# Expert stage with gathered tokens and returned rows by indirect DMA, experts interleaved, and four more weight tiles

## The chip, the cores and the metric

One Trainium2 chip (trn2), one of its cores. The metric is device time in microseconds (us) of one execution. Engines are named as in the profile: PE (TensorE products), PEld (its weight loads), DVE (VectorE), ACT (ScalarE), POOL (GpSimd), SP (SyncE, which issues most DMAs).

## The reference

Two transformer blocks on 512 tokens of 1024 features in fp32. Block 1 mixes by convolution, neighbourhood attention and a gated delta net, and then has a mixture of experts; block 2 has attention and a feed-forward layer. The change lies in the experts of block 1. Of `_hier_moe`, cut to what matters (the last lines in words):

```python
pg = jax.nn.softmax((xt @ wg + bg), axis=-1)            # 4 groups
grp = jnp.argmax(pg, axis=-1)
el_grp = (xt @ we + be).reshape(n, 4, 8)[own group]     # 8 experts of a group
top_logit, top_e = lax.top_k(el_grp, 2)
gate = pg_top * jax.nn.softmax(top_logit, axis=-1)
# of each token's two experts e: y += gate * ((silu(x @ w1[e]) * (x @ w3[e])) @ w2[e])
```

There are 32 experts, w1 and w3 of 1024x512 and w2 of 512x1024. Each of the 512 tokens goes to two experts.

## The kernel before, in words

The expert stage runs from about 474 to 1054 us of the trace. The work of the experts is cut into blocks of 64 token slots. The first four experts (`NPRE`) have one block each at the start; of the others 26 have one block (a unit of 64 slots) and two have two (a unit of 128 slots). Which expert takes which block is a list that the kernel computes at run time from the router; four blocks, 256 slots, are a group (`group`, L1279; `seq_g` gives the groups' order). A loop for tokens beyond the listed blocks (`beyond`, L1574) stands before the seventh group and has no turn here.

Weights come as tiles of 1 MB (128x2048 fp32): two of w1, two of w3 and two of w2 for each expert, 192 in all, issued by SP (`issue`, L1337) in the order in which they are used. Each goes into the next buffer of a ring: three tiles of tag `s`, five of tag `t`, and later two `u`; `WSEQ` gives the ring's order and `U_AT` where `u` comes in. Twelve tiles are loaded ahead, some in memory that is used otherwise later (`pre_issue`, L1363). A load waits until PE has done with what its buffer held.

A group's tokens reach their slots by products. `fill_xs` (L1311) compares each slot's number with the slot keys `K` of the 512 tokens (two keys a token, one for each expert), which gives a one-hot matrix `oh`; for each of eight feature tiles eight products of `oh` with the normed tokens `hN` (in two parts, hi and lo) give the transposed inputs, and `evac_x` puts scale and shift of the norm on them (alternately on DVE and ACT).

An expert (`expert`, L1396) runs two halves of 16 products for w1 and w3 (the unit's inputs are the stationary operand), the SiLU gate (`sil` on ACT, `ge` on DVE), four transposes of `ge`, the copy `gT` on ACT, and 16 products with w2. `evac_y` (L1442) multiplies the result by the gate and a row `G2` and splits it in two parts, `Yh` and `Yl`. The results go back to the tokens by products too: `slot_side` (L1427) makes the one-hot matrix `S` of a pair of units (128 slots), and `scatter_steps` (L1452) runs 16 products of `S` with `Yh` and `Yl` for each pair, whose sums DVE adds to the tokens (`xb`; `big` in the trace), eight steps a pair.

`run_pair` (L1471) sets the order: it runs the two units of a pair one after the other and puts the steps of the next group's inputs and of the last pair's return at fixed places between an expert's parts; the tables `PLAN0` to `PLAN3` say how many at each place. In the last pair a one-element square root (`warm`) has ACT load its table early. Behind the stage stands the norm of block 2: `begin` multiplies the tokens by a row (`xc`), and PE transposes them.

Of the kernel before, what the change touches and what calls it, by code (L numbers as in the profile page):

```python
# [11 lines left out]
I32 = mybir.dt.int32  # L12
# [12 lines left out]
NS, NS2, NS3 = 3, 5, 2                                    # weight tiles: at all times, from the experts on, and late  # L25
XLAG = 2                                                 # tiles of w_out between x1 and its turning
NPRE = 4                                                 # experts that come first, whatever their load
NOV = 2                                                  # experts that get twice the slots
NSG = NE - NPRE - NOV                                    # the others
NB = NSG + 2 * NOV                                       # blocks of 64 slots after the first NPRE  # L30
seq_g = [0, 4, NSG - 2, 8, NSG + 2, 12, 16, 20]          # their groups, the experts with two blocks in turn with others
NLOOP = 6                                                # group of blocks that the loop comes before
LASTP = 22                                               # first block of the last pair
# the experts' weight tiles in the order of their first use (s, t: NS, NS2; x: slots; u: NS3, from the tiles U_AT on)
WSEQ = "sssttttt" + "xx"
U_AT = (11, 12)
# steps of the pair before (outputs' way back) and of the next group (slots) before the four quarters of an expert: the
# first and the second pair, a pair's first and second expert, an expert of two blocks
PLAN0 = [(0, 2), (0, 4), (0, 0), (0, 0)]
PLAN3 = [(0, 1), (0, 1), (4, 2), (4, 2)]  # L40
PLAN2 = [[(0, 1), (0, 0), (2, 1), (2, 1)], [(0, 0), (0, 0), (2, 1), (2, 1)]]
PLAN1 = [(0, 1), (0, 2), (4, 3), (4, 3)]
# [34 lines left out]

TILES = order_tiles(ORD)

# [68 lines left out]
def kernel(ctx: ExitStack, tc: tile.TileContext, a: dict, out, dbg=None, stop=99):  # L148
# [965 lines left out]
    if stop <= 1:  # L1114
        cmn.close()
        return
# [1236 lines left out]
```

## Time and profile before

| | us |
|---|---|
| median of 3 runs | 1889.21 (1883.33 to 1890.45) |
| span of the profiled execution | 1882.1 |
| its own time around the span | not given |
| first expert product to the end of the last one | 473.76 to 1054.11 |
| first transposes of block 2 | 1068.08 |

The profiled execution's span is that from its first to its last instruction; the runs' times hold some launch and end around it. The page's busy shares are averages over both blocks; the stage that the change touches is read by its own windows.

### The profile page before, as it was taken

The numbers are of one execution on the slowest core, as the hardware profiler recorded it, in microseconds if no ns is written. First come the engines' busy times: TensorE is split into PE (matmuls) and PEld (weight loads), VectorE is DVE, ScalarE is ACT, GpSimd is POOL, SyncE is SP. The second block draws the span as 40 slices with busy tenths as digits, with TensorE's granted clock in tenths as the row PEclk, the third lists the DMA queues.
The fourth block names the chain that finished last, engine by engine and source line by source line (L and its number), as shares of the span: only waits on it lengthen the run. The fifth ranks groups of instructions, "written<-read, shape, count | busy, mean of one in ns | idle before, by whom it ended". The sixth has DMA issues, their size and how long they took to land.

```text
span 1882.1 us, 22777 instructions
## 1 busy us (share of the span) xinstructions
PE 1745.2 (93%) x8346; PEld 1208.8 (64%) x8346; DVE 1053.9 (56%) x1959; ACT 683.5 (36%) x1355; POOL 497.6 (26%) x460
## 2 busy tenths in 40 slices
PE   4978989997999999999899799999999999999998
PEld 3757767775444445454443386866688778888886
DVE  7866777764455243544533678755436765425545
ACT  4454543443211111111121554656533454314432
POOL 4364523203111111111111232233202432322251
PEclk7989999998999999999999899999999999999999
DMA  7636234564689887978898457412133332232221
GB/s 286 198 120 218 84 131 136 201 239 188 270 352 401 322 319 270 369 288 326 330 426 349 149 199 262 167 61 86 45 112 117 119 104 104 84 112 90 92 99 45
DMA packets 90177, 370.20 MB, mean 197 GB/s; under 512 B 19680, under 2 KB 42704, under 8 KB 49744
## 3 DMA queue, kind: packets, MB, share of 16 engines
q1 hardware_dynamic: 90064, 368.72, 53.1%
q8 instruction: 67, 1.10, 0.2%
q14 instruction: 46, 0.38, 0.1%
HBM read 359.23 MB, written 9.46 MB: 196 GB/s over the span
## 4 chain that ended last, share of the span: by engine, by line
PE 42%; DVE 4%; ACT 2%; DMA 1%; issue 1%; POOL 1%; DVEq 0%; SPq 0%; ACTq 0%; POOLq 0%
PE b L186 37%; PE b L1906 1%; PE b L1807 1%; PE b L1894 1%; DVE adascr L189 1%; DMA ws<-in_wada_dram 1%; DVE big L192 1%; ACT junk L1634 0%; ACT wh L342 0%; DVE wl L192 0%; PE b L1731 0%; DVE big L189 0%; DMA crow<-in_crow_dram 0%; PE b L2100 0%; POOL hF L192 0%
## 5 line engine op out<-in xcount | busy, mean ns | idle before, releaser
L186 PE MATMUL b<-ws,xs 128*64 128x512 f32 (+1 forms) x896 | 253.2, 595 | 2.0 <-DVEq L1583 2.0
L192 POOL TENSOR_TENSOR wl<-ws,wh 128x1024 fp32r<-128x1024 f32 (+1 forms) x60 | 142.7, 2380 | 377.6 <-ACT wh L342 360.8
L342 ACT CAST wh<-ws 128x1024 fp32r<-128x1024 f32 (+1 forms) x154 | 151.8, 993 | 219.8 <-PE b L186 182.7
L192 POOL TENSOR_TENSOR Yl<-y,Yh 64x512 fp32r<-64x512 f32 (+1 forms) x60 | 77.7, 1315 | 479.0 <-ACT Yh L342 479.0
L186 PE MATMUL b<-hF,wh 128*128 128x512 f32 x656 | 202.2, 389 | 0.0
L186 PEld LDWEIGHTS b<-ws,xs 128*64 128x64 f32 (+1 forms) x896 | 85.3, 140 | 152.1 <-issue 149.3
L192 DVE TENSOR_TENSOR wl<-ws,wh 128x1024 fp32r<-128x1024 f32 (+1 forms) x94 | 115.9, 1237 | 90.7 <-ACT wh L342 87.6
L186 PE MATMUL b<-hB,wh 128*128 128x512 f32 x512 | 164.3, 401 | 0.0
L192 DVE TENSOR_TENSOR big<-big,b 128x512 f32<-128x512 f32 x136 | 89.3, 683 | 114.2 <-PE b L186 113.4
L189 DVE SCALAR_TENSOR_TENSOR adascr<-ws,crow 128x1024 bf16<-128x1024 f32 x96 | 135.6, 1412 | 9.0 <-DMA ws<-in_wada_dram 8.0
L186 PEld LDWEIGHTS b<-hF,wh 128*128 128x128 f32 x656 | 123.1, 188 | 25.5
L186 PE MATMUL b<-hT,wh 128*128 128x512 f32 x384 | 132.8, 424 | 0.0
L186 PE MATMUL b<-ws,gT 128*64 128x512 f32 (+1 forms) x496 | 122.1, 606 | 6.5 <-ACT gT L1416 6.5
L186 PE MATMUL b<-hF,wl 128*128 128x512 f32 x328 | 127.6, 389 | 0.0
L186 PEld LDWEIGHTS b<-hB,wh 128*128 128x128 f32 x512 | 96.7, 193 | 23.5 <-issue 1.8
L189 DVE SCALAR_TENSOR_TENSOR u<-b,cols,u 128x511 f32<-128x511 f32 x88 | 65.8, 748 | 79.3 <-ACT u L2181 77.8
L189 DVE SCALAR_TENSOR_TENSOR y<-b,gsl,G 64x512 f32<-64x512 f32 (+1 forms) x64 | 48.0, 750 | 98.6 <-PE b L186 66.6
L186 PE MATMUL b<-hB,wl 128*128 128x512 f32 x256 | 101.6, 397 | 0.0
L342 ACT CAST Yh<-y 64x512 fp32r<-64x512 f32 (+1 forms) x64 | 39.5, 617 | 169.1 <-DVE y L189 169.1
L186 PEld LDWEIGHTS b<-oh,hN 128*128 128x128 f32 x576 | 77.2, 194 | 20.2 <-issue 16.5
L186 PE MATMUL b<-wh,gf 128*128 128x512 f32 x288 | 88.7, 389 | 0.0
L1409 ACT ACTIVATE sil<-b 64x512 f32<-64x512 f32 (+1 forms) x32 | 18.9, 591 | 189.8 <-PE b L186 189.8
(483 smaller groups left out, 3433.9 us busy)
## 6 DMA issues: line engine op xcount, KB each, us to landing
ws<-in_ew_dram SPq DMA_DIRECT2D x188, 1024.0 KB, 7.3
ws<-in_wada_dram SPq DMA_DIRECT2D x48, 1024.0 KB, 5.0
ws<-in_w_upT_dram SPq DMA_DIRECT2D x22, 1024.0 KB, 4.9
ws<-in_w_in2T_dram SPq DMA_DIRECT2D x16, 1024.0 KB, 4.8
ws<-in_w_inT_dram SPq DMA_DIRECT2D x12, 1024.0 KB, 5.1
ws<-in_w_downN_dram SPq DMA_DIRECT2D x8, 1024.0 KB, 4.9
ws<-in_w_outT_dram SPq DMA_DIRECT2D x4, 1024.0 KB, 4.8
ws<-in_w_v_dram SPq DMA_DIRECT2D x4, 1024.0 KB, 5.2
```

Source lines behind the costliest of these rows:

```text
L186: nc.tensor.matmul(o, l, r, start=start, stop=stop)
L189: return nc.vector.scalar_tensor_tensor(o, i0, s, i1, op0=op0, op1=op1, **kw)
L192: (eng or nc.vector).tensor_tensor(o, i0, i1, op)
L342: nc.scalar.copy(hi, src)
L1409: nc.scalar.activation(s_, b[0][r[0], :], AF.Silu)
L1807: nc.tensor.matmul(o[j], x_[k][:, t], w_[:, i], start=k == 0 and n == 0 and j % 2 == 0, stop=k == KT - 1 and n == 2, skip_group_check=True)
L1894: nc.tensor.transpose(tp[:, k * P:(k + 1) * P], sp[:, k * P:(k + 1) * P], ident)
L1906: nc.tensor.matmul(po[64 * g_:64 * g_ + 64, k * P:], v[k][:, 64 * h:64 * h + 64], PT[g_][:, PO[k]:PO[k] + T - k * P], start=k == 0, stop=k ...
```

## The change

Token vectors move by indirect DMAs. The normed tokens are written to DRAM (`ud`) by ACT's queue. `fill_xs` compares slots and keys as before (eight compares, one for each key), but multiplies the one-hot matrices by columns of two numbers only: 16 small products for a group give each slot's token number and its row in the return buffer. DVE turns them into integers, POOL's queue gathers 128 rows of 4 KB for each half of a group (`xg`; empty slots lie out of bounds and are skipped), and PE transposes the tile, 16 transposes a group.

Results are only multiplied by `G2` into a tile `Y`, which POOL's queue scatters to `yd` in DRAM (`send`), a pair at a time. Near the end `come_back` reads `yd` in four 1 MB tiles on POOL's queue, and eight DVE steps add gate times row to the tokens. The last pair still goes through `S` and products. The loop for tokens beyond the list moves to the same scheme.

Units are interleaved (`run`): a unit's first half, then the previous unit's transposes of `ge`, the unit's second half, then the previous unit's w2 products. The w2 tiles are issued one unit later (`order_w`). The ring has 13 tiles that are used in turn (five `t`, one `k`, three `s`, four new `e`), one more (`x`) that is used once, and later two `u`; 14 tiles are loaded ahead. The early square root is left out. `PLAN_F` says where a unit's place holds steps of the next group's inputs.

```diff
-WSEQ = "sssttttt" + "xx"
-U_AT = (11, 12)
...
+NE4 = 4
+NLATE = 11
+WSEQ = "tttttkxssseeee"
+U_AT = (15, 16)
+PLAN_F = {0: [(0, 0, 0, 0), (0, 1, 1, 0), (1, 1, 1, 1), (1, 1, 1, 1)],
+          4: [(1, 0, 1, 0), (0, 0, 0, 0), (1, 1, 1, 1), (1, 1, 1, 1)],
+          3: [(1, 0, 1, 0), (1, 1, 1, 1), (1, 1, 1, 1)],
+          1: [(1, 1, 0, 4)]}
...
+    ud = dpool.tile([T, D], F32, name="ud")
+    yd = dpool.tile([2 * T, D], F32, name="yd")
...
+    xg = [EX.tile([P, D], F32, name="xg%d" % h) for h in range(2)]
...
-            nc.scalar.activation(u, v, AF.Copy, scale=rs[:, j:j + 1])
-            split(hi, lo, u, nc.gpsimd)
+            nc.scalar.activation(u, xb[:, j, f_], AF.Copy, scale=rs[:, j:j + 1])
+            nc.scalar.dma_start(ud[j * P:(j + 1) * P, f_], u)
...
-    def fill_xs(slots, xs):
-        oh = c4("oh", [P, NTT, 256])
+    def fill_xs(slots, xs, nh, r_, np_, ix):
+        w = nh * P
+        oh = [EX.tile([P, NTT, 256], F32R, tag="oh", name=nm("oh"), bufs=2) for _ in range(2)]
         for j in range(NTT):
-            t = M.tile([P, 256], F32, tag="oht", name=nm("oht"), bufs=2)
-            ts_(t, slots, K[:, 1, j:j + 1], None, OP.is_equal)
-            last[0] = stt(oh[:, j], slots, K[:, 0, j:j + 1], t, OP.is_equal, OP.add)
+            for i in range(2):
+                ts_(oh[i][:, j, :w], slots[:, :w], K[:, i, j:j + 1], None, OP.is_equal)
+        yield
+        n = r_.shape[3]
+        b = bank()[:, :2 * n].rearrange("p (h n) -> p h n", h=2)
+        for h in range(nh):
+            for j in range(NTT):
+                for i in range(2):
+                    mm(b[:, h], oh[i][:, j, h * P:(h + 1) * P], r_[:, j, i], j == 0 and i == 0, j == NTT - 1 and i == 1)
...
+        nc.vector.tensor_copy(sc[:, :nh], b[:, :nh])
+        ts_(e[:, :nh], sc[:, :nh, 0], 0.0, 4096.0, OP.is_equal, OP.mult)
+        stt(gi[:, :nh], sc[:, :nh, 0], -1.0, e[:, :nh], OP.add, OP.add)
+        tt(e[:, :nh], e[:, :nh], sc[:, :nh, 1], OP.add)
+        last[0] = stt(ri[:, :nh], sc[:, :nh, 0], -1.0, e[:, :nh], OP.add, OP.add)
+        ix["ri"], ix["sc"] = ri, sc
+        for h in range(nh):
+            nc.gpsimd.indirect_dma_start(out=xg[h][:np_], out_offset=None, in_=ud[:, :],
+                                         in_offset=bass.IndirectOffsetOnAxis(ap=gi[:np_, h:h + 1], axis=0),
+                                         bounds_check=T - 1, oob_is_err=False)
         yield
...
-            for j in range(NTT):
-                for q in range(2):
-                    mm(b, hN[q][j][m // 4][:, (m % 4) * P:(m % 4 + 1) * P], oh[:, j], j == 0 and q == 0,
-                       j == NTT - 1 and q == 1)
-            evac_x(xs[:, m], b, m)
+            w = (nh - 1) * P + np_
+            for h in range(nh):
+                nc.tensor.transpose(b[:, h * P:h * P + np_], xg[h][:np_, m * P:(m + 1) * P], ident[:np_, :np_])
+            evac_x(xs[:, m, :w], b[:, :w], m)
             yield
...
+    def send(Y, ri, h, np_=P):
+        nc.gpsimd.indirect_dma_start(out=yd[:, :], out_offset=bass.IndirectOffsetOnAxis(ap=ri[:np_, h:h + 1], axis=0),
+                                     in_=Y[:np_], in_offset=None, bounds_check=2 * T - 1, oob_is_err=False)
...
+        skip += "e" if nis[0] > 6 * NE - NLATE else ""
...
+    def order_w(us_):
+        for i, u in enumerate(us_):
+            for q in range(2):
+                yield from wreq(u, q)
+            if i:
+                yield from wreq(us_[i - 1], 2)
+        yield from wreq(us_[-1], 2)
...
+    def evac(b, Y, r):
+        for q in range(2):
+            f_ = slice(q * 512, (q + 1) * 512)
+            tt(Y[r, f_], b[q], G2[r, f_], OP.mult)
...
+    def results(u, b):
+        ps_, r = u["pair"], u["rows"]
+        if u["last"]:
+            if "Y" not in ps_:
+                ps_["S"], ps_["Y"] = slot_side(made[ps_["grp"]][2]["sc"][:, ps_["h"]]), \
+                    [EX.tile([P, D], F32R, tag="oh", name=nm("Yp"), bufs=2) for _ in range(2)]
+            evac_y(b, *ps_["Y"], ps_["S"][1], r)
+            if r.stop == P:
+                late.append((*ps_["Y"], ps_["S"][0]))
+            return
+        if "Y" not in ps_:
+            ps_["Y"] = out_tile()
+        evac(b, ps_["Y"], r)
+        if r.stop == P:
+            send(ps_["Y"], made[ps_["grp"]][2]["ri"], ps_["h"])
+    def run(us_):
+        prev = None
...
+        for u in us_:
+            h = u.get("hook", lambda i: None)
+            h(0)
+            x = expert(u["xs"](), u["sl"], u)
             next(x)
-            if leng is None and i == 1:
-                tc.keep_in_program_order(nc.scalar.activation(small.tile([P, 1], F32, tag="warm", name=nm("warm")),
-                                                              ones[:, 0:1], AF.Sqrt))
...
+            h(1)
+            if prev:
+                next(prev[1])
+            h(2)
+            next(x)
+            h(3)
+            if prev:
+                results(prev[0], next(prev[1]))
+                if "after" in prev[0]:
+                    prev[0]["after"]()
+            prev = u, x
+        end(prev)
...
+    def come_back():
+        for j in range(NTT):
+            t = EX.tile([P, 2048], F32, tag="we", name=nm("yb"), bufs=NE4).rearrange("p (i f) -> p i f", i=2)
+            nc.gpsimd.dma_start(t, yd.rearrange("(i j p) f -> j p i f", i=2, j=NTT)[j])
+            for i in range(2):
+                stt(xb[:, j], t[:, i], gt[:, i, j:j + 1], xb[:, j], OP.mult, OP.add)
...
+    flat_us[-5]["after"] = zero_rows
+    flat_us[-3]["after"] = come_back
+    run(flat_us[n0:])
```

The order of instructions moves on PE, on POOL and at the stage's end on DVE.

On PE the first unit of before alternates its w1 (`kg`) and w3 (`ws`) products on its inputs (`xf`):

```order
L186 MATMUL b_4069<-kg_3997,xf_3995 64x512
L186 MATMUL b_4070<-ws_3999,xf_3995 64x512
L186 MATMUL b_4069<-kg_3997,xf_3995 64x512
L186 MATMUL b_4070<-ws_3999,xf_3995 64x512
L186 MATMUL b_4069<-kg_3997,xf_3995 64x512
```

In the middle of the program, now, a unit runs them in fours (`x4`), and the transposes of gathered tokens (`xg`) and of the previous unit's `ge` stand between its two halves:

```order
L188 MATMUL b_4956<-we_4968,xs_4442 64x512 x4
L188 MATMUL b_4957<-ws_1141_4970,xs_4442 64x512 x4
L1365 MATMUL b_4980<-ident,xg_3993 128x128
L1365 MATMUL b_4980<-ident,xg_3994 128x128
L1459 MATMUL b_4984<-ident,ge_4932 128x64 x4
L1365 MATMUL b_4991<-ident,xg_3993 128x128
L1365 MATMUL b_4991<-ident,xg_3994 128x128
```

Of the 30 units of 64 slots, 17 alternated before, 9 ran in fours and 4 were mixed; now 10 alternate and 20 run in fours.

On POOL before, the start of the expert stage held the splits of normed tokens (`hN`) and of results (`Yl`):

```order
L192 TENSOR_TENSOR hN_3962<-xr_3991,hN_3954 128x512
L192 TENSOR_TENSOR Yl_4255<-y_4256,Yh_4254 64x512
L192 TENSOR_TENSOR Yl_4255<-y_4260,Yh_4254 64x512
L192 TENSOR_TENSOR Yl_4255<-y_4303,Yh_4254 64x512
L192 TENSOR_TENSOR Yl_4255<-y_4307,Yh_4254 64x512
```

On POOL now, the same place holds the gathers (`ud` by the indices `gi`) and the sends (a pair's `y` to `yd` by `ri`):

```order
L1307 MEMSET xg_3994 128x1024
L1357 DMA xg_3993<-ud,gi_4080 128x1024
L1357 DMA xg_3994<-ud,gi_4080 128x1024
L1357 DMA xg_3993<-ud,gi_4269 128x1024
L1357 DMA xg_3994<-ud,gi_4269 128x1024
L1371 DMA yd<-y_3997,ri_4081 1024x1024
L1357 DMA xg_3993<-ud,gi_4503 128x1024
L1357 DMA xg_3994<-ud,gi_4503 128x1024
L1371 DMA yd<-y_4437,ri_4081 1024x1024
```

Both kinds stand in one queue: a send behind the next group's gathers where its results come later.

At the end of the stage DVE before had the last pair's sums in pairs of steps (`big<-big,b`) around the two evacuations of the last unit (`y`):

```order
L192 TENSOR_TENSOR ge_8007<-sil_8006,b_7981 64x512
L192 TENSOR_TENSOR big<-big,b_8027 128x512
L192 TENSOR_TENSOR big<-big,b_8031 128x512
L189 SCALAR_TENSOR_TENSOR y_8049<-b_8035,gsl_7921,G_3495 64x512
L189 SCALAR_TENSOR_TENSOR y_8053<-b_8036,gsl_7921,G_3495 64x512
```

Now the eight sums of the returned rows (`yb`) stand there, the first two ahead of the last unit's `ge` and the others ahead of or between the evacuations of the last pair (`y`, split into `Yp`):

```order
L191 SCALAR_TENSOR_TENSOR big<-yb_6878,gt,big 128x1024 x2
L194 TENSOR_TENSOR ge_6938<-sil_6937,b_6895 64x512
L198 TENSOR_SCALAR S_6955<-tokr,sc_6462 128x512
L191 SCALAR_TENSOR_TENSOR big<-yb_6882,gt,big 128x1024 x2
L191 SCALAR_TENSOR_TENSOR big<-yb_6886,gt,big 128x1024 x2
L191 SCALAR_TENSOR_TENSOR big<-yb_6890,gt,big 128x1024
L191 SCALAR_TENSOR_TENSOR y_6961<-b_6941,gsl_6957,G_3536 64x512
L191 SCALAR_TENSOR_TENSOR big<-yb_6890,gt,big 128x1024
L194 TENSOR_TENSOR Yp_6960<-y_6961,Yp_6959 64x512
```

The last unit's `ge`, and with it its transposes and w2 products, now stands behind the first read of returned rows on DVE. Behind the stage the order on every engine is as before.

## Rows read from the trace of the kernel before

**Rows 1.** Windows of the expert stage, with two stretches inside it.
```profile
core 0: us, PE busy (x) PEld busy (x) DVE busy (x) ACT busy (x) POOL busy (x), PEclk, DMA share, GB/s
474.00:1055.00 581.00, 554.72 (x2481) 259.11 (x2477) 256.73 (x479) 92.83 (x169) 77.74 (x60) 1.00 0.85 330
540.00:620.00 80.00, 77.78 (x379) 36.55 (x374) 37.69 (x67) 12.74 (x23) 13.01 (x10) 1.00 1.00 402
940.00:1000.00 60.00, 58.72 (x282) 25.84 (x280) 23.14 (x41) 10.47 (x19) 10.00 (x8) 1.00 1.01 426
```

**Rows 2.** Waits of SP's queue, whole span: us in total, times, longest.
```profile
SPq L182 <- PE b L186: 415.1, 151, 12.7
```

**Rows 3.** Groups of PE by form, 440 to 1075: busy us, mean ns | idle.
```profile
L186 PE MATMUL b<-ws,xs 128*64 128x512 f32 x832 | 225.0, 595 | 2.0 <-DVEq L1583 2.0
L186 PE MATMUL b<-ws,gT 128*64 128x512 f32 x464 | 108.0, 607 | 6.5 <-ACT gT L1416 6.5
L186 PE MATMUL b<-oh,hN 128*128 128x256 f32 x576 | 82.7, 290 | 2.4 <-DVE oh L189 2.4
L186 PE MATMUL b<-Yh,S 128*128 128x512 f32 x136 | 59.8, 441 | 3.0 <-ACT Yh L342 3.0
...
L186 PE MATMUL b<-ws,xf 128*64 128x512 f32 x112 | 28.9, 596 | 0.0
...
L1414 PE MATMUL b<-ident,ge 64*128 64x64 f32 x120 | 13.8, 235 | 14.1 <-DVE ge L192 13.0
...
L186 PE MATMUL b<-sel,pls 128*128 128x36 f32 x8 | 1.1, 279 | 0.0
L260 PE MATMUL b<-ident,K 128*128 128x128 f32 x8 | 1.0, 272 | 0.0
```

**Rows 4.** Timeline of PE in two units: start us, us, instructions.
```profile
494.38 7.03 PE L186 MATMUL b<-ws,xf 128*64 128x512 f32 x32
...
665.28 5.37 PE L186 MATMUL b<-ws,xs 128*64 128x512 f32 x16
...
672.66 5.42 PE L186 MATMUL b<-ws,xs 128*64 128x512 f32 x16
```

**Rows 5.** Timeline of the stage's start, DVE and PE.
```profile
466.77 0.62 DVE L196 TENSOR_SCALAR oht<-pat,K 128x256 f32<-128x256 f32 x2
...
467.92 5.91 PE L186 MATMUL b<-oh,hN 128*128 128x256 f32 x32 [2.44 <-DVE oh L189]
...
473.76 0.64 PE L186 MATMUL b<-kg,xf 128*64 128x512 f32 x1
```

**Rows 6.** Timeline of PE at the stage's end.
```profile
1050.46 3.65 PE L186 MATMUL b<-ws,gT 128*64 128x512 f32 x16
...
1057.91 0.40 PE L186 MATMUL b<-Yh,S 128*128 128x512 f32 x1
...
1058.37 0.40 PE L186 MATMUL b<-Yh,S 128*128 128x512 f32 x1
...
1068.08 1.97 PE L1644 MATMUL b<-ident,xc 128*128 128x128 f32 x8 [7.72 <-ACT xc L1695]
```

**Rows 7.** DMA issues, whole span: KB each, median us from issue to landing.
```profile
ws<-in_ew_dram SPq DMA_DIRECT2D x188, 1024.0 KB, 7.3
...
xd<-zero SPq DMA_DIRECT2D x8, 256.0 KB, 6.3
...
U<-gd SPq DMA_DIRECT2D x4, 64.0 KB, 2.6
```

**Rows 8.** Groups of DVE and ACT, 440 to 1100: busy us, mean ns.
```profile
L189 DVE SCALAR_TENSOR_TENSOR xc<-big,frow 128x1024 f32<-128x1024 f32 x4 | 6.8, 1690 | 0.0
...
L1492 ACT ACT_TABLE_LOAD x1 | 1.3, 1283 | 0.0
```

More of the change, by code (lines that the diff above doesn't have):

```diff
@@ L408, in c4 @@
     def c4(name, shape, dt=F32R):
-        return CN.tile(list(shape), dt, tag="w4", name=nm(name), bufs=2 * NW)
+        return c4p[1].tile(list(shape), dt, tag="w4", name=nm(name), bufs=2 * NW)
     def csplit(src, shape, leng=None):
@@ L1394, with expert @@
         dump("gt", gt)
-    def expert(xs, sl, w1s, w3s, w2s, wexp=wexp, side=lambda i: None):
+    def expert(xs, sl, u, wexp=wexp):
         n = sl.stop - sl.start
@@ L1506, in static @@
-    def static(e):
-        return lambda: [[a[n][e, q] for q in range(2)] for n in ("ew1", "ew3", "ew2")]
-    listed = {}
-    def pair(xs, i, p, fill=iter(())):
-        units = [lambda q=q: listed.get(q) or dyn(q) for q in ((p, p + 1) if p < NSG else (p,))]
-        run_pair(xs, 2 * CAP * i, kco[:, p // 2:p // 2 + 1], units, fill, leng=None if p == LASTP else nc.gpsimd)
+    def results(u, b):
[13 more added lines that the diff above has]
+            send(ps_["Y"], made[ps_["grp"]][2]["ri"], ps_["h"])
@@ L1569, in rows_, with beyond @@
         st3[0] = moe.enter_context(tc.tile_pool(name="stream3", bufs=NS3, reuse_waits="tile"))
-        key_rows()
         for i in range(2):
-            nc.scalar.copy(kg["G"][:, i, :], bc_rows(gt[:, i, :]))
-    def beyond(p):
-        scatter(*late.pop())
-        for e in range(2):
-            w1s, w3s, w2s = listed[p + e] = dyn(p + e)
-            for src in (w1s[0], w3s[0], w1s[1], w3s[1], *w2s)[:NS + NS2 - 6 * e]:
-                ahead.append(issue(src, "u"))
+            g_ = small.tile([P, NTT], F32, tag="gr", name=nm("gr"))
+            nc.scalar.copy(rtg[:, :, i, 2], gt[:, i, :])
+            tt(g_, gt[:, i, :], f32v(rtg[:, :, i, 2]), OP.subtract)
+            nc.vector.tensor_copy(rtg[:, :, i, 3], g_)
+    def beyond(nxt_us):
+        for src, _ in zip(order_w(nxt_us), range(len(WSEQ) - 1)):
+            ahead.append(issue(src, "u"))
         if a.get("_over", True):
@@ new lines, in beyond @@
+                for _ in range(3):
+                    next(x)
+                Y = out_tile()
+                evac(next(x), Y, slice(0, CAP))
+                send(Y, ix["ri"], 0, CAP)
+    groups = [[{"w": static(e), "n": CAP} for e in range(NPRE)]]
+    for p0 in seq_g:
+        g_ = []
+        for p in range(p0, min(p0 + 4, NB)):
+            if p < NSG:
+                g_.append({"w": lambda p=p: dyn(p), "n": CAP})
+            elif (p - NSG) % 2 == 0:
+                g_.append({"w": lambda p=p: dyn(p), "n": P})
+        groups.append(g_)
@@ new lines, with hook, steps @@
+    made = {0: (xs, fill0, ix)}
+    def hook(g_, i):
+        def steps(q):
+            if g_ == 0 and i == 0:
+                if q == 2:
+                    run_all(made[0][1])
+                if q == 3:
+                    rows_()
+                return
+            if i == 0 and q == 1:
+                run_all(made[g_][1])
+            k = g_ + 1
+            n = PLAN_F[len(groups[g_]) if g_ else 0][i][q]
+            if k < len(groups) and n:
+                if k not in made:
+                    made[k] = group(seq_g[k - 1])
+                for _ in range(n):
+                    next(made[k][1], None)
+        return steps
@@ new lines, with zero_rows @@
+    for n, g_ in enumerate(groups):
+        at = 0
+        pairs = [{"grp": n, "h": h} for h in range(2)]
+        for i, u in enumerate(g_):
+            u["xs"] = lambda n=n: made[n][0]
+            u["sl"] = slice(at, at + u["n"])
+            u["rows"] = slice(at % P, at % P + u["n"])
+            u["pair"] = pairs[at // P]
+            u["last"] = n == len(groups) - 1 and at >= P
+            u["hook"] = hook(n, i)
+            at += u["n"]
+    def zero_rows():
+        z = out_tile()
+        nc.gpsimd.memset(z, 0.0)
+        send(z, made[len(groups) - 1][2]["ri"], 1)
@@ new lines, in come_back @@
+    def come_back():
+        for j in range(NTT):
+            t = EX.tile([P, 2048], F32, tag="we", name=nm("yb"), bufs=NE4).rearrange("p (i f) -> p i f", i=2)
+            nc.gpsimd.dma_start(t, yd.rearrange("(i j p) f -> j p i f", i=2, j=NTT)[j])
+            for i in range(2):
+                stt(xb[:, j], t[:, i], gt[:, i, j:j + 1], xb[:, j], OP.mult, OP.add)
+    flat_us = [u for g_ in groups for u in g_]
+    n0 = sum(len(g_) for g_ in groups[:1 + NLOOP])
+    run(flat_us[:n0])
+    beyond(flat_us[n0:])
@@ L1654 @@
     if stop <= 4:
-        scatter(*late.pop())
+        scatter(*late.pop(), range(NTT))
         dump("x2n", xb)
         moe.close()
-        ya.close()
+        ex_.close()
         cmn.close()
@@ L1774 @@
     ya.close()
+    c4p[0].close()
     cmn.close()
```

178 lines of the change are left out of this document (69 added, 109 removed).

## The prediction

> **What bounds the kernel now.** I first read the windows of the expert stage [rows 1]. From 474 to 1055 us TensorE (PE) is busy for 554.7 of 581 us at a granted clock of 1.00 (the 2.4 GHz level), while the DMA engines stand at a share of 0.85 and 330 GB/s. So the products set the pace. The queue's own waits say the same: SP, which loads the weights, waited 415.1 us in all for PE to release a tile [rows 2]. The reader should also see how near the second limit is: over 80 us the transfers made 402 GB/s at a share of 1.00, over 60 us 426 at 1.01 [rows 1]. The weights are 192 tiles of 1.0486 MB, so cutting PE's work runs the stage into that limit.
>
> Next I read PE's groups by form [rows 3]: which products the change takes out. Then its timeline [rows 4], because the price of the first products depends on their order: a unit whose w1 and w3 products alternate runs its 32 in 7.03 us; where four of one follow four of the other, 16 take 5.37 us, so 32 take 10.79 with the second half's 5.42. Finally the beginning and end of the stage, whose first expert product starts at 473.76 [rows 5] and whose last ends at 1050.46 + 3.65 = 1054.11, with the first transpose of block 2 at 1068.08 [rows 6].
>
> **PE's work, part by part.** The stage is 1054.11 − 473.76 = 580.4 us.
> - One-hot products for the inputs go: 576 for 82.7 us [rows 3], of which 5.91 [rows 5] lie ahead of the first expert product: −76.8.
> - The return's products go, for 16 of 17 pairs. A Yh and a Yl product follow each other's start at 0.46 us per pair of them (1057.91 to 1058.37 [rows 6]); 128 such pairs: −59.
> - With the units interleaved, PE need not wait for ge (14.1) and gT (6.5) [rows 3], since another unit's products stand between: −20. If that product is itself waiting for weights, this cover is gone; that case is in the second limit.
> - The order of the 30 units of 64 slots changes. By the two orders, 17 alternate before and 9 run in fours (4 are mixed); after it, 10 alternate and 20 run in fours. First products now cost 225.0 + 28.9 = 253.9 [rows 3]; then 10 × 7.03 + 20 × 10.79 = 286.1: +32. This part of the cost is not in the description, only in the order.
> - Transposes of the gathered tiles come: 136, by the nearest form at 1.0/8 = 0.125 us (ident,K [rows 3]): +17. Index products of two columns: 136, nearest sel,pls at 1.1/8 = 0.14: +19. Bounds for both kinds: 0.06 (half, as fewer columns) to 0.27 (a lone one's mean); 16 to 73 us together. I take the row's pipelined price, since they are issued in runs.
>
> Sum: 580.4 − 76.8 − 59 − 20 + 32 + 17 + 19 = 493 us.
>
> **The start.** The first tokens need a new chain after the slot keys at 466.77 [rows 5]: 8 compares at 0.31 (2.5), 16 index products (2.2), five small VectorE steps at about 0.3 (1.5), the gather, and 16 transposes with their evacuation (2.0). For the gather nothing in this trace is issued by GpSimd; the nearest are 64 KB in 2.6 us and 1 MB in 7.3 under load [rows 7]. I take 6, as its 512 KB a tile lies nearer the upper. That gives about 481, +7 against 473.76. The write of the normed tokens (256 KB each; such a one landed in 6.3 [rows 7]) begins before the keys are ready, so I cost it at nothing. PE's own end is then 481 + 493 = 974.
>
> **The second limit.** 14 tiles are loaded ahead, so 178 × 1.0486 = 186.6 MB follow from about 484.5, when the first half of the first unit releases tiles. New traffic: 512 tokens with two experts each are 1024 rows of 4 KB, 4.2 MB (rows of empty slots are skipped): gathers without the first group's 3.7 MB, sends without the last pair's 4.0, the read back 4.2: 12 MB. 198.6 MB at 402 GB/s is 494 us: 978.5, plus the last tile's landing and its products (2 + 3.65): 984. At 426 it would be 466 us: 956, so PE's 974 would stand. I take 402, the rate over the longer window, and so 985. The four more tiles move this little: they cover more of an uneven stretch, not more bytes.
>
> Against that rate speaks a rule of the Trainium skill, "DMA: Bandwidth & Descriptors", section "Where 436 GB/s comes from": for loads from HBM the memory side, about 358 GB/s per core, binds, not the fabric's 435. By it the same bytes would take an estimated 555 us. The windows at 402 and 426 GB/s [rows 1] disagree with it for this kernel.
>
> **Gathers later on.** Each group's indices and gather are issued inside the previous group. By the new order, PE has work of about 7, 22, 22, 7, 25, 7, 25 and 14 us between a group's index products and its first transposes. Small steps plus a gather: 1.5 + 2.6 to 1.5 + 7.3, so 4 to 9 us: waits of 0 to 6 us over the stage; I take 0, because the weights are the limit then.
>
> **The end.** The returned rows are read back and summed in eight VectorE steps ahead of the last pair's evacuation. A send (6.3), a read of 1 MB (7.3) [rows 7] and 8 × 1.69 (xc<-big,frow, the same shape [rows 8]) make 27 us from the last sent pair's evacuation. PE covers it with 5.4 + 5.4 + 3.65 + 3.65 of the last two units, 18 us. The rest, +8, delays the last pair's evacuation. The square-root table load that was issued early comes back on the path: +1.3 [rows 8]. The end of the stage to the first transpose of block 2 is thus 14.0 + 9.3.
>
> The first transpose of block 2: 985 + 14 + 9.3 = 1008, −60 against 1068.08. Nothing behind it is moved. The profiled span is 1882.1, so 1822; the profiled execution's own time outside the span is not shown, but the runs' 1883.33 to 1890.45 lie 1.2 to 8.4 above it. The median 1889.2 − 60 gives **1829 us**. What this kernel's measurement can tell from no change is about 0.5%: below 1879.8 or above 1898.7.
>
> **Rivals.**
> - *PE alone bounds* (chance 0.12): transfers hold 426 GB/s and the sums hide. 974 + 14 + 1.3 = 989: −79, **1810**. For it: share 1.01 for 60 us. Against it: the stretch at 402.
> - *Both limits take turns* (0.15): tiles are late in some units and PE is behind in the units run in fours, so the mean is midway between the present 330 and the peak 426, 378 GB/s: 198.6 MB take 525 us: 1010 + 6, so +30: **1859**. For it: SP must still wait for releases in a unit's order.
> - *The transfers hold their peak only in stretches* (0.06): the mean rises a quarter of the way from 330 to 426, to 354 GB/s. 198.6 MB take 561 us: 484.5 + 561 + 6 + 23 = 1075, +7: **1896**, no change that can be told. The two windows speak against it, the mean of 330 does not, as PE set it. The rule of the page cited above would give about this.
> - *Gathers come late, slower than before* (0.08). GpSimd issues them while VectorE is busy for 257 of 581 us [rows 1]; if its issue waits for VectorE, the chain from index products to transposes grows, and all of PE's in-order queue stands behind the transposes. Set against the covers above, a chain of c us costs the sum of c − cover: 71 us at 25 us, which eats the gain (1054 − 974 − 9.3 = 71); 111 at 30 us. PE would then end at 1085, the transposes of block 2 start at 1108: +40, **1929**. It decides from about 25 us, over three times the 7.3 us of a loaded megabyte; no row is near that.
>
> On this last mechanism the Trainium skill, "SBUF — State Buffer", section "SBUF: two separate sides", warns that GpSimd cannot write the descriptors of its DMAs while VectorE runs a two-port operation such as an fp32 copy. No row of this trace shows such a DMA, so it stays a rival.
>
> **Chances.** Forecast 0.59; with the two other fast cases faster has 0.86, same 0.06, slower 0.08. The range reaches from PE alone, with the start's bound some 5 us lower (1804), to the turn-taking case and a little of its start and index bounds (1862); the last two rivals, 0.14, lie outside.
>
> **What would show it.** Right: PE's busy time in the stage falls to about 470 to 480 us of some 505, transfers rise to about 400 GB/s at a share near 1, SP's waits for PE shrink from 415 us, and the idle time before first products names late weights. Transposes of xg should wait for nothing over a few us, the first expert product should stand near 481 and the first block-2 transpose near 1008. Wrong: idle before the xg transposes of tens of us (gathers late), w1 and w3 products over 290 us, or a stage rate still near 330 to 360 GB/s.

## The result and the profile after

The changed kernel takes 1833.45 us (median of 4 runs, 1831.1 to 1835.4) against 1887.28 of the kernel before (4 runs): a ratio of 0.9722, 95% interval 0.9703 to 0.974. The prediction was 1829, range 1804 to 1862. The profiled span is 1830.7 us, 51.4 less than before.

Windows of the changed kernel, from the first expert product to the end of the last, whole and in parts:

```profile
core 0: us, PE busy (x) PEld busy (x) DVE busy (x) ACT busy (x) POOL busy (x), PEclk, DMA share, GB/s
476.00:1002.00 526.00, 488.62 (x1917) 186.50 (x1915) 120.80 (x259) 51.05 (x103) 36.37 (x37) 0.95 0.95 384
476.00:540.00 64.00, 58.01 (x265) 22.10 (x263) 18.18 (x47) 8.99 (x17) 3.08 (x3) 0.90 0.85 345
540.00:600.00 60.00, 60.00 (x248) 23.47 (x249) 13.99 (x33) 5.89 (x12) 4.09 (x4) 1.00 1.01 420
840.00:900.00 60.00, 48.81 (x206) 18.04 (x206) 11.59 (x28) 5.64 (x12) 4.01 (x4) 0.89 0.88 338
960.00:1002.00 42.00, 26.85 (x96) 8.96 (x92) 15.76 (x17) 3.06 (x6) 3.87 (x5) 0.80 0.79 318
```

Against [rows 1] the stage is 55 us shorter, and the transfers' mean rose from 330 to 384 GB/s. In 540 to 600 both limits are full at once: PE is busy 60 of 60 us and the DMA share is 1.01 at 420 GB/s. The mean stays lower because of holes at the start, around the loop and at the end, and there PE's granted clock is also below 1.00.

PE's groups of the changed kernel by form, 440 to 1050 us (busy, mean ns | idle before, releaser), which answer to [rows 3]:

```profile
L188 PE MATMUL b<-ws,xs 128*64 128x512 f32 x600 | 210.0, 606 | 11.2 <-DMA ws<-in_ew_dram 11.2
L188 PE MATMUL b<-ws,gT 128*64 128x512 f32 x360 | 117.5, 633 | 4.4 <-ACT gT L1461 4.4
...
L1365 PE MATMUL b<-ident,xg 128*128 128x128 f32 x136 | 27.6, 305 | 20.0 <-DMA xg<-ud,gi 20.0
...
L188 PE MATMUL b<-rt,oh 128*128 128x2 f32 x120 | 17.1, 268 | 1.6 <-DVE oh L198 1.6
...
L1459 PE MATMUL b<-ident,ge 64*128 64x64 f32 x120 | 14.0, 238 | 10.7 <-DVE ge L194 10.7
```

The 13.0 us that PE waited for ge in many small pieces [rows 3] have become one wait of 10.7 at the end; there are 20.0 us of waits for gathers (9.0 of them the first) and one of 11.2 for weights behind the loop. In that one the transfers run dry (a DMA share of 1.01 from 870 to 874 us, 0.06 from 878 to 880, and PE goes on at 880.24), so it is a hole for both limits. SP's waits, whole span, against [rows 2]:

```profile
SPq L184 <- PE b L188: 298.4, 112, 17.4
SPq L184 <- DMA ws<-in_ew_dram: 39.0, 23, 2.5
SPq L184 <- PE b L1365: 37.7, 23, 4.2
```

The last line is the waits for PE's new transposes: with them SP's waits for PE fell from 415.1 to 336.1 us.

DMA issues of the changed kernel (median us to landing), against [rows 7]:

```profile
ws<-in_ew_dram SPq DMA_DIRECT2D x130, 1024.0 KB, 12.3
...
yb<-yd POOLq DMA_DIRECT2D x4, 1024.0 KB, 12.2
...
xg<-ud,gi POOLq DMA_INDIRECT x17, 8.5
yd<-y,ri POOLq DMA_INDIRECT x17, 8.3
```

A weight tile now lands 12.3 us after its issue, not 7.3, while the rate rose: so more tiles are under way at once.

Timeline of the start on DVE, ACT, POOL and PE, which answers to [rows 5]:

```profile
461.38 2.18 DVE L198 TENSOR_SCALAR oh<-pat,K 128x256 fp32r<-128x256 f32 x8
...
466.52 0.16 DVE L191 SCALAR_TENSOR_TENSOR ri<-sc,se 128x2 int32<-128x2 f32 x1
466.87 0.33 ACTq L1314 DMA_DIRECT2D ud<-xr  x1
469.84 1.29 POOL L1357 DMA_INDIRECT xg<-ud,gi  x1 [20.11 <-DVE l L1579]
474.69 1.97 PE L1365 MATMUL b<-ident,xg 128*128 128x128 f32 x8 [8.99 <-DMA xg<-ud,gi]
476.70 4.75 PE L188 MATMUL b<-ws,xs 128*64 128x512 f32 x16
```

Timeline of the end on DVE and PE, which answers to [rows 6]:

```profile
984.21 2.60 DVE L191 SCALAR_TENSOR_TENSOR big<-yb,gt,big 128x1024 f32<-128x1024 f32 x2 [17.75 <-DMA yb<-yd]
986.73 0.68 DVE L194 TENSOR_TENSOR ge<-sil,b 64x512 f32<-64x512 f32 x1
987.47 0.69 PE L1459 MATMUL b<-ident,ge 64*128 64x64 f32 x4 [10.74 <-DVE ge L194]
995.79 6.26 PE L188 MATMUL b<-ws,gT 128*64 128x512 f32 x16 [4.42 <-ACT gT L1461]
1016.11 1.97 PE L1737 MATMUL b<-ident,xc 128*128 128x128 f32 x8 [6.48 <-ACT xc L1791]
```

The last unit's ge waits on DVE behind the first sum, and that sum for the read back. The last w2 product ends at 1002.05 and block 2 begins 14.06 us later (13.97 before).

### The profile page after: what moved, and what is told of

It reads as the page before. It is cut to its first block, busy times and chain, and to the rows that moved or that the text cites. A ratio compares the mean times of both kernels' runs of the same rounds, so it can differ in the third digit from the quotient of the medians.

```text
span 1830.7 us, 21487 instructions
## 1 busy us (share of the span) xinstructions
PE 1680.2 (92%) x7770; PEld 1137.4 (62%) x7770; DVE 916.7 (50%) x1803; ACT 639.7 (35%) x1284; POOL 453.0 (25%) x433
## 4 chain that ended last, share of the span: by engine, by line
PE 43%; DVE 4%; DMA 2%; ACT 2%; issue 1%; POOL 0%; DVEq 0%; ACTq 0%
PE b L188 37%; PE b L2003 1%; PE b L1904 1%; PE b L1991 1%; PE b L1827 1%; DVE big L191 1%; DMA ws<-in_wada_dram 1%; DVE adascr L191 1%; DMA ws<-in_ew_dram 1%; ACT junk L1727 0%; DVE big L194 0%; DMA yb<-yd 0%; DMA frow<-in_fnrow_dram 0%; PE b L2197 0%; POOL hF L194 0%
## 5 line engine op out<-in xcount | busy, mean ns | idle before, releaser
L188 PE MATMUL b<-ws,xs 128*64 128x512 f32 (+1 forms) x648 | 233.3, 607 | 11.2 <-DMA ws<-in_ew_dram 11.2
L188 PEld LDWEIGHTS b<-ws,xs 128*64 128x64 f32 (+1 forms) x648 | 73.8, 143 | 126.7 <-issue 123.2
L188 PE MATMUL b<-ws,gT 128*64 128x512 f32 (+1 forms) x392 | 131.8, 630 | 4.4 <-ACT gT L1461 4.4
L188 PE MATMUL b<-we,xs 128*64 128x512 f32 (+1 forms) x304 | 112.1, 637 | 0.0
L194 DVE TENSOR_TENSOR ge<-sil,b 64x512 f32<-64x512 f32 (+1 forms) x32 | 22.1, 689 | 161.3 <-PE b L188 112.7
L1371 POOL DMA_INDIRECT yd<-y,ri x17 | 16.9, 994 | 319.2 <-DVE y L194 293.4
L188 PE MATMUL b<-hT,wl 128*128 128x512 f32 x192 | 79.6, 415 | 9.4 <-POOL wl L194 4.7
L1319 ACT ACTIVATE xs<-b,mods,ab 128x256 f32<-128x256 f32 (+1 forms) x36 | 19.4, 550 | 175.7 <-PE b L1365 174.8
L188 PEld LDWEIGHTS b<-hT,wh 128*128 128x128 f32 x384 | 71.3, 197 | 15.1 <-issue 2.8
## 6 DMA issues: line engine op xcount, KB each, us to landing
ws<-in_ew_dram SPq DMA_DIRECT2D x130, 1024.0 KB, 12.3
```

The costliest lines, as they stand in the source:

```text
L188: nc.tensor.matmul(o, l, r, start=start, stop=stop)
L194: (eng or nc.vector).tensor_tensor(o, i0, i1, op)
L1319: nc.scalar.activation(o, b, AF.Identity, scale=A, bias=B)
L1371: nc.gpsimd.indirect_dma_start(out=yd[:, :], out_offset=bass.IndirectOffsetOnAxis(ap=ri[:np_, h:h + 1], axis=0), in_=Y[:np_], in_offset=No ...
```

## The experiments

Times below are set against the changed kernel through both kernels' ratios to the kernel before; by those intervals such a difference is good to about 5 us.

**Two limits: bytes, order, both.** The first run leaves one weight tile in six out:

```diff
-        return [w[0][q], w[1][q]] if q < 2 else list(w[2])
+        return [w[0][q], w[1][q]] if q < 2 else [w[2][0]]
```

> The changed kernel with only the first of an expert's two w2 tiles loaded and used for both halves of the w2 products: 32 of 192 weight tiles (33.6 MB) are left out, all products stay. Theory A, the weights' transfers set the pace of the changed stage: 33.6 MB at 0.41 MB per us would give 82 us, until PE's own 488 us of work bind; 25 to 38 us less than the changed kernel (about 1796 to 1808). Theory B, PE's own work in its order sets the pace (it is busy 60 of 60 us where the transfers are at a share of 1): only the wait at the loop (11 us) and little else can go; 1822 to 1833.

Ratio 0.9493 (0.9467 to 0.9519), 1790.9 us: 43 less. That is more than theory A's bound and about half of what the bytes would take alone. One of this kernel's windows:

```profile
660.00:720.00 60.00, 60.00 (x217) 24.75 (x218) 12.33 (x29) 5.52 (x11) 4.06 (x4) 1.00 0.89 330
```

From 600 to 780 us PE is busy all the time while the transfers fall to 330 to 388 GB/s: with fewer bytes PE's work sets the pace there. The second run chains each half's products in program order (`ms` are the products just written):

```diff
+            for x0, x1 in zip(ms, ms[1:]):
+                order(x1, x0)
```

> The changed kernel with the w1 and w3 products of each half held to alternate, as the program writes them, so that all 30 units of 64 slots alternate and none runs in fours; nothing else differs. Theory A, transfers set the pace: PE finishes earlier and waits for weights instead; within 8 us of the changed kernel (1825 to 1835). Theory B, PE's order sets the pace: the 32 us that the prediction put on the order come back, at least 20 of them; 1801 to 1813.

Ratio 0.9653 (0.9633 to 0.9673), 1818.7 us: 13 less, between the two theories. Windows of everything that reads xs (476 to 1002), of the changed kernel and of this one, each a row of its own view:

```profile
476.00:1002.00 526.00, 328.00 (x1024) 107.05 (x1024) 18.68 (x36) 19.41 (x36) 0.95 0.95 384
```

```profile
476.00:1002.00 526.00, 269.90 (x1024) 82.87 (x1024) 18.77 (x36) 19.48 (x36) 0.93 0.94 388
```

The first number behind the length is PE's busy time: 58 us of PE's time were the order's. What became of it stands in this kernel's windows, its PE groups, the line of PE behind the loop, and SP's waits (the profiled execution took 1813.8 us, the fastest of the four):

```profile
660.00:720.00 60.00, 58.83 (x225) 22.75 (x227) 12.80 (x29) 5.51 (x11) 4.05 (x4) 0.96 1.01 420
720.00:780.00 60.00, 53.30 (x210) 21.37 (x208) 12.58 (x30) 6.41 (x13) 3.07 (x3) 0.94 1.02 420
```

```profile
L188 PE MATMUL b<-ws,xs 128*64 128x512 f32 x600 | 181.4, 605 | 27.4 <-DMA ws<-in_ew_dram 27.4
...
865.05 1.12 PE L188 MATMUL b<-ws,xs 128*64 128x512 f32 x1 [26.30 <-DMA ws<-in_ew_dram]
...
SPq L184 <- DMA ws<-in_ew_dram: 150.8, 79, 3.2
SPq L184 <- PE b L188: 124.1, 52, 21.8
```

From 540 to 840 us the transfers go on at 419 to 420 GB/s without a hole, and SP's waits for PE's products fell from 298.4 to 124.1 us while those for the landing of weight tiles rose from 39.0 to 150.8: the transfers set the pace there, as theory A has it. PE's own wait for weights is nearly all in one place, 26.3 us behind the loop (11.2 in the changed kernel). It also waits 26.5 us for gathers (20.0) and 19.8 for the last `ge` and `gT` (15.1). With 4.5 more for weights elsewhere, longer waits took about 31 of the 58 us. The third run has both edits:

> Both edits at once: products alternate, and the second w2 tile of each expert is left out. Theory A alone: as with the tile left out alone. Theory B alone: as with the alternation alone. If the two limits stand at the same level, neither edit alone brings much and both together bring 40 to 60 us: 1773 to 1793.

Ratio 0.939 (0.9372 to 0.9408), 1769.5 us: 63 less, a little below the expected 1773 to 1793 and near the 43 + 13 of the two edits (the 7 more are not clear of the noise). If one limit held throughout, one of the two edits would bring nothing. Both bring something, and nearly the sum: the two limits take turns, each setting the pace of some stretches.

**The four tiles.** The ring loses its `e` tiles:

```diff
-WSEQ = "tttttkxssseeee"
-U_AT = (15, 16)
+WSEQ = "tttttkxsss"
+U_AT = (11, 12)
```

> The changed kernel without the four more weight tiles in the ring (they are kept for the read back alone): nine tiles in turn and two later ones, ten loaded ahead. The prediction says the tiles move little, since they cover uneven stretches and change no bytes: 0 to 10 us slower, 1833 to 1843. Rival: the interleaved order holds w2 tiles a unit longer, so that the ring of before is too short for it: over 20 us slower, above 1853.

Ratio 0.9777 (0.9752 to 0.9802), 1843.5 us: 10 more, the upper end of what the prediction's view gives. This run also has nine tiles in place of 13 issued ahead of the loop, and its wait behind the loop is 7.3 us, not 11.2.

**The sums at the end.** The read back stays and the sums move:

```diff
-    flat_us[-3]["after"] = come_back
+    flat_us[-3]["after"] = read_back
+    flat_us[-2]["after"] = come_back
```

(with the sums chained on VectorE behind what was written before them)

> The changed kernel with the eight sums of returned rows moved on VectorE behind the ge of the last unit and the first evacuations of the last pair (the read back is issued where it was). The theory: the 10.7 and 4.4 us that PE waits ahead of the last unit's transposes and w2 products come from those sums, since ge stands behind the landing of the read back; both waits go, but part of the sums then lies ahead of the last evacuation. 4 to 11 us less than the changed kernel, 1822 to 1829. Rival: the read back's landing sets the end either way, because every sum must be done before block 2: 0 to 2 us less.

Ratio 0.9701 (0.9678 to 0.9723), 1826.6 us: 4 less, not clear of the uncertainty, so the time does not tell the theory from its rival. PE's timeline of this kernel says where it went:

```profile
991.84 0.80 PE L188 MATMUL b<-Yp,S 128*128 128x512 f32 x1 [9.65 <-ACT Yp L344]
...
1010.68 1.97 PE L1746 MATMUL b<-ident,xc 128*128 128x128 f32 x8 [5.59 <-ACT xc L1800]
```

Both waits ahead of the last unit are gone. In their place the last pair's products wait 9.65 us, for the evacuation that now stands behind the sums, and 15.2 in all against 1.7 in the changed kernel; block 2 begins 5.4 us earlier, 0.6 of which lie ahead of the stage. The wait moved more than it went.

**Interleaving.** One unit after the other:

```diff
-            if prev:
-                next(prev[1])
             h(2)
             next(x)
             h(3)
-            if prev:
-                results(prev[0], next(prev[1]))
+            next(x)
+            results(u, next(x))
```

(and w2 tiles issued with their own unit)

> The changed kernel with the units one after the other: a unit's w2 products follow its own second half, and its w2 tiles are issued there; the steps of gather, transposes and sends stay. The prediction took 20 us for the waits for ge and gT that the interleaving removes. If those waits lie beside transfers that set the pace, PE waits for ge instead of for weights: 0 to 10 us slower than the changed kernel. If PE's work sets the pace, 15 to 25 us slower, 1848 to 1858.

Ratio 0.9857 (0.9831 to 0.9882), 1856.3 us: 25 more. PE's groups of this kernel (470 to 1030):

```profile
L188 PE MATMUL b<-ws,gT 128*64 128x512 f32 x328 | 85.3, 658 | 8.4 <-ACT gT L1458 8.4
...
L1456 PE MATMUL b<-ident,ge 64*128 64x64 f32 x120 | 14.2, 241 | 40.5 <-DVE ge L194 40.5
```

PE waits 40.5 us for ge where the kernel before waited 13.0 [rows 3]: its one-hot products stood in those gaps. The 25 us are what the interleaving is worth; the rest of these waits does not show in the time.

**The first gather.** The router's exponential is held behind the last write of normed tokens:

```diff
+        order(ex_i.ins, ud_i.ins)
```

> The changed kernel with the last write of normed tokens held ahead of the router's exponential on ScalarE's queue. The theory: the first gather waited for that write (issued at 466.87 us, behind an exponential that waits for VectorE), not for its indices, which were ready at 466.5; the write goes out near 463, the gather near 466.7 and the first expert product near 473.5 in place of 476.7. The time is 2 to 4 us less, at the edge of what can be measured. Rival: GpSimd's issue itself is late, then nothing moves.

Ratio 0.9733 (0.9709 to 0.9756), 1832.3 us: no change, but not by the rival's reason. The second exponential of the router took the first one's place ahead of the write, which still went out at 466.88 us. The run with both held is the last but one below.

**One-hot products back.** Beside each step of transposes eight products of `oh` with itself, results unused:

```diff
+            for t_ in range(8):
+                mm(bd[:, :w], oh[t_ % 2][:, t_ // 2, :P], oh[t_ % 2][:, t_ // 2, :w], t_ == 0, t_ == 7)
```

> The changed kernel with as many one-hot products of 128x256 put back at the places of the transposes as the kernel before had in the stage (544, 76.8 us there); their results are not used, so the output is the same. Theory A, transfers set the pace where PE has slack: 30 to 60 us slower than the changed kernel, PE filling its waits first. Theory B, PE's work sets the pace throughout: 70 to 80 us slower, 1903 to 1913.

Ratio 0.9962 (0.9947 to 0.9977), 1874.7 us: 45 more, within theory A's range and well under theory B's. The steps hold 576 such products, 32 more than were meant, which keep PE busy for 79.4 us and (64 narrower ones) 9.1. So some 88 us of work costs about 45 us here: the rest goes where PE would have waited. What the products of the kernel before were worth is thus about 45 us too, as far as these stand for them.

**The kernel before, alternating.** The edit of the second run on the kernel before:

> The kernel before, with its w1 and w3 products held to alternate in every half; nothing else differs. In its order 21 halves of units run in fours, at 5.4 us against 3.6, so 37 us of PE's work go. If PE's work sets the pace of the kernel before, as the prediction read its rows: 20 to 37 us less than the kernel before, 1850 to 1868. If transfers already set it in most stretches: under 10 us less.

Ratio 0.9874 (0.9854 to 0.9893), 1861.3 us: 24 less than the kernel before, from the order alone, of an estimated 37. PE's work did set its pace, in the main.

**Gathers twice.**

```diff
+            nc.gpsimd.indirect_dma_start(out=xg[h][:np_], out_offset=None, in_=ud[:, :],
+                                         in_offset=bass.IndirectOffsetOnAxis(ap=gi[:np_, h:h + 1], axis=0),
+                                         bounds_check=T - 1, oob_is_err=False)
```

> The changed kernel with each gather issued twice, the second into the same tile behind the first; the extra rows are the same ones. It lengthens the chain from index products to transposes by about 10 us (8.5 to land and 1.3 to issue). By the covers of the prediction the three groups with 7 us pay 10 each, the one with 14 a few, and the start pays 10: 40 us of PE's waits. If those waits were the pace, 1868 to 1876. If transfers, which go on during them, make most of it good: only the start's 10 and a little more, 1843 to 1855. The rival of the prediction, late gathers as the cause of a slower kernel, needs a chain of about 25 us; this one is near 20.

Ratio 0.9908 (0.9885 to 0.993), 1867.9 us: 35 more. Waits of PE in this kernel, 460 to 1000 us:

```profile
PE b L1368 <- DMA xg<-ud,gi: 57.6, 9, 13.6
```

37.6 us more of waits for gathers than in the changed kernel's 20.0, and 35 more in time: a late gather is paid nearly in full, and the transfers do not make it good. The chain grew by less than the 10 us expected: for the second group it takes 18.0 us from the end of the index products to the first transpose (497.84 to 515.79) against 9.8 (493.29 to 503.13), for the first group 13.6 against 9.0.

**Combined.** The edits of the second, fifth and seventh run (with both exponentials held), gathers one place earlier for two kinds of groups, and nine tiles ahead of the loop:

```diff
-PLAN_F = {0: [(0, 0, 0, 0), (0, 1, 1, 0), (1, 1, 1, 1), (1, 1, 1, 1)],
+PLAN_F = {0: [(0, 0, 0, 0), (1, 1, 0, 0), (1, 1, 1, 1), (1, 1, 1, 1)],
...
-          3: [(1, 0, 1, 0), (1, 1, 1, 1), (1, 1, 1, 1)],
+          3: [(1, 1, 0, 0), (0, 1, 1, 1), (1, 1, 1, 2)],
...
-        for src, _ in zip(order_w(nxt_us), range(len(WSEQ) - 1)):
+        for src, _ in zip(order_w(nxt_us), range(9)):
```

> The changed kernel with five edits: w1 and w3 products alternate; the sums of returned rows behind the last ge; both exponentials of the router behind the last write of normed tokens on ScalarE; gathers of the groups with the shortest cover issued one place earlier; nine tiles in place of 13 issued ahead of the loop. If each brings what its wait in the trace or its own run shows (14, 4, 3, 4 and 6 us): 31 us less than the changed kernel, 1796 to 1808. If transfers at their full rate are the floor after the alternation, the other four bring little: 1812 to 1820.

Ratio 0.9608 (0.9589 to 0.9628), 1810.0 us: 21 less than the changed kernel, the fastest that computes everything. Timeline of this kernel on DVE, ACT, POOL and PE:

```profile
458.30 2.18 DVE L198 TENSOR_SCALAR oh<-pat,K 128x256 fp32r<-128x256 f32 x8
459.07 0.33 ACTq L1314 DMA_DIRECT2D ud<-xr  x1
464.11 1.28 POOL L1357 DMA_INDIRECT xg<-ud,gi  x1 [17.45 <-DVE fl L198]
468.95 1.94 PE L1365 MATMUL b<-ident,xg 128*128 128x128 f32 x8 [6.33 <-DMA xg<-ud,gi]
...
850.40 1.11 PE L188 MATMUL b<-ws,xs 128*64 128x512 f32 x1 [16.86 <-DMA ws<-in_ew_dram]
```

The first transposes come 5.7 us earlier, but 3.1 of that is not the edits': the first compare, too, stands at 458.30 in place of 461.38. The other 2.7 are the write's: it goes out ahead of the exponentials, at 459.07 in place of 466.87, and the gather starts 0.7 us behind the start of the last index step (463.45) in place of 3.3. So the write was what the first gather waited for. Behind the loop PE waits 16.9 us, more than in the changed kernel but less than the 26.3 with alternation alone. For gathers beyond the first it waits 12.4 us, against 17.9 with alternation alone and 11.0 in the changed kernel. So against the alternating kernel, which is the right base here, both waits are shorter; together with the other edits that brings 8 to 9 us of the 17 expected. From 540 to 840 us the rate is 414 to 421 GB/s in every window of 60 us. This agrees with the expectation's second theory, transfers as the floor, whose 1812 to 1820 was missed by 2 us.

**GpSimd busy again.**

```diff
+            tt(y_first[0][:, f_], u, u, OP.subtract, nc.gpsimd)
```

> The changed kernel with eight subtractions of 128x512 on GpSimd put back where the kernel before split the normed tokens (their result is overwritten later). The slot keys were ready 5.4 us earlier in the changed kernel (first compare at 461.38 against 466.77 us), which no step of the prediction had. The theory: VectorE's small steps on the router (0.29 us each in the changed kernel) took up to 1.2 us while GpSimd ran its splits; with GpSimd busy again those beside its work take about 1 us and the first compare comes at 464 to 467. Rival: the keys are earlier for another reason (ScalarE's casts are gone as well), and the first compare stays near 461.5. The time itself moves by under 6 us.

Ratio 0.9765 (0.9745 to 0.9785), 1838.6 us: 8 more, where under 6 were expected, and good only to about 5. The profiled execution took 1831.4 us, so its timeline shows the order of the steps but not where the 8 us lie. In it the first transposes start 3 us later (477.68 against 474.69). DVE's timeline of this kernel, then of the changed one, from the first step of the router's norm to the keys:

```profile
451.25 0.16 DVE L200 TENSOR_SCALAR rs<-b 128x4 f32<-128x4 f32 x1 [2.46 <-PE b L188]
...
456.80 1.01 DVE L191 SCALAR_TENSOR_TENSOR fm<-fm,rows 128x128 f32<-128x128 f32 x1
457.85 0.29 DVE L1256 TENSOR_REDUCE ix<-fm 128x4 f32<-128x128 f32 x1
...
464.42 2.18 DVE L198 TENSOR_SCALAR oh<-pat,K 128x256 fp32r<-128x256 f32 x8
```

```profile
452.57 0.16 DVE L200 TENSOR_SCALAR rs<-b 128x4 f32<-128x4 f32 x1 [2.46 <-PE b L188]
...
456.40 0.29 DVE L191 SCALAR_TENSOR_TENSOR fm<-fm,rows 128x128 f32<-128x128 f32 x1
456.72 0.29 DVE L1256 TENSOR_REDUCE ix<-fm 128x4 f32<-128x128 f32 x1
```

From that first step to the first compare it is 13.2 us with GpSimd busy and 8.8 in the changed kernel (to 461.38, above); 452.16 to 466.77, 14.6, in the kernel before. The theory holds for 4.4 of the 5.8 us between the kernel before and the changed one; the rest is open.

## Why the prediction was right, step by step

The time came out within 5 us (54 us gained, 60 forecast), the sign and the main exchange as forecast: PE's one-hot work went, the stage ran into the weights' transfers, and part of the rest of the gain was cut off there. But the sum has errors that offset each other, and one of its own signs of being wrong came true.

- **What bounded the kernel before: right.** Alternation alone gave it 24 of 37 us.
- **The start: 481 forecast, 476.70 measured.** The chain from the keys to the first product took 15.3 us (461.38 to 476.70) against the 14.2 that the terms make, with 3.3 of waiting for the last write, which the prediction had cost at nothing (indices ready at about 466.5, gather at 469.84). It was the keys themselves that came 5.4 us earlier. No step had that. GpSimd's splits, which are gone, account for 4.4 us by the last run; the rest is open.
- **The order of w1 and w3: right in kind, too small.** Forecast +32. The view of xs gives 328.0 us; the same view gave 256.8 of the stage before, with 28.7 for the first group's inputs beside it, so +42, part of it at a lower clock. "Over 290 us" for these products was a sign of being wrong, and it came true: about 31 of the 328.0 are the two units of 128 slots, which the forecast's 286 left out, so some 297 stand against it. The run with alternation shows the price of all fours to be 58 of busy time but 13 of time.
- **Transposes and indices.** 27.6 us for transposes against 17, 17.1 + 1.9 for the index products against 19.
- **Interleaving: right.** Forecast −20; without it 25 us are lost, for waits of another make-up: before, one-hot products lay in them.
- **Transfers: the level right, the mean wrong.** 420 GB/s where nothing is missing, 402 taken; but the mean is 384 (389 from 484.5 us, where the prediction's sum begins), nearer the 378 of the rival in which both limits take turns, at a chance of 0.15. That rival's mechanism is what the runs show, though its time, 1859, was too long. Taking the larger of two ends, 974 and 985, was the step that failed: by the forecast's own figures PE and transfers were within 11 us of each other, so each hole of one was lost to the other. The runs say it most plainly: PE's work taken away brings 13 of 58, bytes taken away 43 of an estimated 82, both 63; PE's work added costs 45 of some 88.
- **Gathers: 0 taken, 11.0 us measured** in four waits of 1.7 to 3.4, beyond the first group's; "nothing over a few us" holds for these, not for the first group's 9.0. A gather lands in 8.5 us, above the 7.3 taken as the upper bound. The run with doubled gathers gives the rival its price: a chain some 8 us longer (second group) cost 37.6 us of waits, 35 in time; at that slope (an estimate) the gain of 54 us would be gone with a chain some 12 us longer than the 9.8 measured, near 22 where the prediction put 25. That the Trainium skill's warning on GpSimd's descriptors ("SBUF — State Buffer", section "SBUF: two separate sides") was at work does not show: each of the 34 indirect DMAs took GpSimd 0.97 to 1.29 us, with DVE busy for 121 of 526 us. No run tests it apart.
- **The end: +8 forecast, 15.1 measured** as 10.7 + 4.4, ahead of the last w2 products and not behind them; behind them nothing was added (14.06 against 13.97), so the table load's 1.3 does not show.
- **The four tiles: "move little" was right, at the edge:** 10 us, a fifth of the gain.

In sum the last w2 product ended at 1002.05 against 993 forecast (985 + 8), block 2 began at 1016.11 against 1008, and the span is 8.7 us longer than the 1822 forecast. That the time is only 4.5 off is in part luck: the forecast took its 60 us from a median that lies 7.1 us above the profiled span of before, and the changed kernel's median lies 2.8 above its own. Two slips of 1 us cancel (984 is carried on as 985, and 27 − 18 as 8). PE's busy time, 488.6 of 526 us, is above the 470 to 480 of 505 that were to be seen; SP's waits, the rate and the late weights came as said, the last only behind the loop.

The rule of the Trainium skill weighed ahead of the result ("DMA: Bandwidth & Descriptors", section "Where 436 GB/s comes from", about 358 GB/s for loads from memory) does not bind this kernel, which runs on one core, either: 410 to 421 GB/s in the four windows from 540 to 780 us.

## What to carry to other kernels

When a change takes away the work of one limit, work out where the other stands, and if the two ends lie within a few per cent, do not take the larger: price each hole (first fill, a loop's drain, a late gather) on top of it. Read the new order of instructions for changes that the description does not name; here it cost 58 us of PE's busy time and 13 us of time. A short run with bytes taken away, one with work taken away and one with both tell in three numbers which limit holds, or that both take turns. Compare a run of several edits with the run of the largest edit alone, and take the start of the stage off both timelines first.

## What the hardware showed that was not expected

**A wait costs more than its length, through the clock.** Behind the loop PE stood still for 11.2 us; windows of the changed kernel around it:

```profile
869.00:880.00 11.00, 0.06 (x2) 0.00 (x0) 1.38 (x2) 0.00 (x0) 0.97 (x1) 0.61 0.80 320
880.00:884.00 4.00, 3.76 (x10) 1.24 (x12) 2.61 (x9) 0.00 (x0) 0.00 (x0) 0.50 0.71 242
884.00:888.00 4.00, 4.00 (x24) 2.19 (x20) 0.00 (x0) 0.00 (x0) 0.00 (x0) 0.87 0.90 317
888.00:892.00 4.00, 4.00 (x22) 1.42 (x23) 0.93 (x6) 0.25 (x1) 2.06 (x2) 1.00 0.90 375
```

The granted clock (the number ahead of the DMA share) was 0.50, the 1.2 GHz level, for the first 4 us behind the wait, and a product took 1.06 us there against 0.59 later. The 16 last w2 products, behind a wait, took 6.26 us at a granted clock of 0.58, against 3.65 [rows 6]. In the kernel before, where no wait of PE's between 470 and 1030 us was over 2.0 us, the stage's clock was 1.00 in the mean [rows 1].

**VectorE's steps with two inputs are slower beside GpSimd's.** 1.01 us against 0.29 for the same step, in the last run, while a reduction with one input kept its 0.29. A step of the same kind that began at 458.89, while GpSimd stood still (458.70 to 458.95), kept its 0.29 too. The Trainium skill, "SBUF — State Buffer", section "SBUF: two separate sides", says that GpSimd and VectorE share a pair of ports as an exclusive lock, which a VectorE operation with two inputs from that memory needs against a GpSimd operation that reads it. The rows agree; that the lock is the cause was not tested apart.
